# One scheduling block around a four-stage hybrid backbone kernel: its order is laid out on the library's timeline machine

## The chip, the cores and the metric

The kernel runs on one core of one Trainium2 chip. The metric is device time in microseconds (us), the median of several executions. One execution was also recorded by the hardware profiler; its rows are shown further down. Engines: PE is TensorE (matmuls), PEld its weight loads, DVE is VectorE, ACT is ScalarE, POOL is GpSimd, SP is SyncE, which issues the DMAs here.

## What is computed

Two layers (DEPTH = 2) act on 1024 latent tokens and 256 context tokens, width 1024, one sample, all float32.

```
h  = rmsnorm(x, g_pre) * (1 + scale) + shift      # adaLN; shift, scale, gate from silu(c) @ w_mod
layer 0: u = [ diff_attention(8 heads, 1280 keys) * silu(gate) ,  b * short_conv(c * h') * silu(gate) ]
layer 1: u = [ neighbourhood_attention(16 heads, 8x16 window + 256 context keys) * silu(gate) ,
               gated_linear_attention(4 heads, both directions) * silu(gate) ]
x  = x + gate * rmsnorm(u @ w_out, g_post)
```

Every product with a weight is done as three float32r matmuls on high and low parts (hi*hi, hi*lo, lo*hi), so that PE has much more to do than any other engine.

## The kernel before

`Kernel.run` calls the stages one after another: `setup` and `start` (conditioning, first norm, `h`), `layer0` (eight heads of differential attention, `diff_head`), `out0` (output projection and the second norm), `layer1` (gated linear attention, GLA, for four heads in `gla_head`, then neighbourhood attention, `na`, for 16 heads), and `out1` (last output projection).

The wide projections are cut in units of 1024 x 128 weights. A `Stream` hands them out: `ws.run(1)` inside an attention stage emits one projection step (24 matmuls into one of two PSUM buffers, `proj_chunk`, L445) between two pieces of attention work. That work is the cover: while a chain of small instructions runs on DVE, ACT and POOL, PE has a projection to go on with. Each weight unit is loaded by a DMA (L234), rounded on ACT (`whi`, L251), and its remainder is formed on POOL or DVE (`wlo`, L252).

What sets the order. The program is traced in the order in which the Python code emits it, and each instruction gets that place as its priority; `high_priority(offset=n)` moves what is emitted in it n places forward, a negative n back. When the context closes, the tile library plays the program on a timing simulator of the core: whenever an engine can take an instruction, it gets, of those whose operands and buffers are ready in the simulation, the one with the earliest priority. The order found this way becomes the fixed queue of each engine, with semaphores between the queues; on the chip each engine goes through its own queue in that order and waits where an operand is late. So the simulator's prices are not the time of anything on the chip, but they decide which of two instructions stands first in a queue. An order that was right at the simulator's prices makes an engine wait on the chip where an operand takes longer than priced.

The library has two such simulators. The default one is used for the kernel before; the library says of it that it leaves out the fixed cost of GpSimd's elementwise instructions. The other, the timeline machine, is described as the more detailed of the two, and recommended for a phase whose length GpSimd decides; its list of devices holds a read port and a write port that GpSimd and VectorE share. Both take an activation table as already loaded.

Three places carry offsets by hand: the K and Q products of the GLA levels (-6), the query split of the neighbourhood attention (`nqd`, +60) and the split of its turned probabilities (`pth`, `ptl`, -20). Only the last stage has an order of its own: in `out1` the queue of units is drained in `tc.manual_schedule()`, where every engine keeps the order of the code.

The GLA stage works on one head at a time. `gla_levels` goes through seven levels for each of the groups of tokens; a level exponentiates (ACT, L1138), multiplies K on POOL and Q on DVE (L1140), multiplies the two on PE (`gl`, L1145), and merges the result on DVE (L1154), while DVE updates the running sums (L1149). `gla_chunk` then carries the state S from chunk to chunk: a transpose, its high and low parts (`gkh` on ACT, `gkl` on DVE, L1205), the update `gu` (L1212) and the output `go` (L1229) on PE.

Of the kernel before, what the change touches and what calls it, by code (L numbers as in the profile page):

```python
# [40 lines left out]
class Stream:  # L41
# [39 lines left out]
    def run(self, n):  # L81
        for _ in range(n):
            if not self.step():
                return
# [15 lines left out]
class Kernel:  # L100
# [6 lines left out]
        return (ctx or self.ctx).enter_context(self.tc.tile_pool(name=name, bufs=bufs, **kw))  # L107

    def run(self):
        self.setup()  # L110
        with ExitStack() as es:
            self.hp = self.pool("hp", ctx=es)
            rope_es, out_es = ExitStack(), ExitStack()
            self.start(rope_es)
            conv_es = self.layer0(rope_es)
            self.layer1(self.out0(conv_es, out_es), out_es)
            with ExitStack() as es2:
                self.out1(es2)
# [1501 lines left out]
```

## Time and profile before

| | |
|---|---|
| median of 3 runs | 3096.65 us (3096.41 to 3098.51) |
| the profiled execution, its own time | 3092.35 us |
| its span, first to last instruction | 3090.6 us |
| granted PE clock, mean | 0.992 |
| instructions | 42514 |

The profile page gives the busy time of each engine, and the trace behind it answers by stretch, by tile, or by who waited for whom. A busy engine is not one at its peak: the ends of matmuls are modelled. An idle engine off the critical path costs nothing.

### The profile page before, as it was taken

To read this page: it belongs to the slowest core of one execution; us is meant where nothing else is said; L and a number is where in the kernel's file an instruction comes from. 1 tells how busy PE (TensorE), PEld (TensorE's weight loads), DVE (VectorE), ACT (ScalarE), POOL (GpSimd) and SP (SyncE) were. 2 spreads that over 40 slices of the span, in tenths; PEclk is the share of its full clock that TensorE was granted. 3 is DMA by queue.
4 is the path that set the end of the run, shared out by engine and by line. 5 is a ranking of instruction groups with operands and counts; after the bars stand their busy time and mean duration, and the time that the engine had idled before them with its cause. 6 is when DMAs were issued, how large, how long until landed. Compare 5 with 4: busy or idle time off the path is not lost. (4 is left out here: it accounts for less than half of the span.)

```text
span 3090.6 us, 42514 instructions
## 1 busy us (share of the span) xinstructions
PE 2935.1 (95%) x16244; PEld 2437.7 (79%) x16244; DVE 1909.9 (62%) x3276; ACT 1498.9 (48%) x2757; POOL 1025.9 (33%) x813
## 2 busy tenths in 40 slices
PE   6999999999999999999999998989899999999898
PEld 4788888888888888888877777778777888887686
DVE  5575757566565657565244778685836666667723
ACT  4453535354445445453344555555535555556522
POOL 2203130313021221205233334342435555556622
PEclk9999999999999999999999999999999999999999
DMA  6011111211020211116342112111131111113323
GB/s 227 28 51 50 49 45 35 65 34 54 28 72 28 65 35 42 43 50 208 96 159 81 42 42 63 48 55 59 52 99 31 47 49 44 43 44 98 117 77 123
DMA packets 236982, 206.59 MB, mean 67 GB/s; under 512 B 43591, under 2 KB 194538, under 8 KB 236778
## 3 DMA queue, kind: packets, MB, share of 16 engines
q1 hardware_dynamic: 236778, 203.87, 21.3%
q8 instruction: 128, 2.10, 0.3%
q14 instruction: 76, 0.62, 0.1%
HBM read 168.17 MB, written 35.67 MB: 66 GB/s over the span
## 5 line engine op out<-in xcount | busy, mean ns | idle before, releaser
L252 POOL TENSOR_TENSOR wlo<-wraw,whi 128x1024 fp32r<-128x1024 f32 x149 | 366.8, 2462 | 1075.6 <-ACT whi L251 994.9
L445 PE MATMUL pj<-hBh,whi 128*128 128x512 f32 (+1 forms) x1712 | 382.2, 352 | 1.4 <-ACT gk L1048 1.0
L445 PE MATMUL pj<-hBl,whi 128*128 128x512 f32 (+1 forms) x1712 | 368.0, 347 | 0.0
L445 PE MATMUL pj<-hBh,wlo 128*128 128x512 f32 (+1 forms) x1712 | 351.3, 344 | 0.0
L251 ACT CAST whi<-wraw 128x1024 fp32r<-128x1024 f32 x176 | 184.4, 1048 | 319.9 <-PE ops L761 190.2
L445 PEld LDWEIGHTS pj<-hBh,wlo 128*128 128x128 f32 x1712 | 277.3, 190 | 36.8
L445 PEld LDWEIGHTS pj<-hBl,whi 128*128 128x128 f32 x1712 | 277.0, 190 | 34.3
L445 PEld LDWEIGHTS pj<-hBh,whi 128*128 128x128 f32 x1712 | 273.0, 190 | 35.4 <-ACT gk L1048 1.2
L445 PE MATMUL pj<-hAh,whi 128*128 128x512 f32 x968 | 279.5, 410 | 18.9 <-ACT ropex L524 12.9
L445 PE MATMUL pj<-hAl,whi 128*128 128x512 f32 x968 | 255.3, 394 | 0.0
L599 DVE TENSOR_REDUCE st<-S 128x1 f32<-128x1280 f32 (+1 forms) x160 | 203.8, 1274 | 79.8 <-PE S L597 79.8
L445 PE MATMUL pj<-hAh,wlo 128*128 128x512 f32 x968 | 249.6, 393 | 0.0
L1451 POOL TENSOR_TENSOR np<-np,nst 128x640 f32<-128x640 f32 x128 | 166.7, 1305 | 192.6 <-DVE nst L1450 141.9
L601 ACT ACTIVATE p<-S,st 128x1280 f32<-128x1280 f32 (+1 forms) x160 | 186.1, 1163 | 85.1 <-DVE st L599 83.6
L445 PEld LDWEIGHTS pj<-hAh,whi 128*128 128x128 f32 x968 | 170.6, 191 | 52.6 <-ACT ropex L524 14.4
L445 PEld LDWEIGHTS pj<-hAh,wlo 128*128 128x128 f32 x968 | 180.4, 188 | 36.6
L445 PEld LDWEIGHTS pj<-hAl,whi 128*128 128x128 f32 x968 | 177.9, 189 | 34.5
L597 PE MATMUL S<-kst,qd 128*128 128x512 f32 (+1 forms) x832 | 193.6, 363 | 4.9 <-ACT p L601 3.5
L597 PEld LDWEIGHTS S<-kst,qd 128*128 128x128 f32 x832 | 137.8, 189 | 45.7 <-ACT p L601 25.2
L1447 DVE CUSTOM_DVE_ANT_0 np<-NS,nB 128x640 f32<-128x640 f32 x128 | 105.3, 823 | 90.5 <-PE NS L1444 84.7
L622 ACT CAST ath<-atr 128x512 fp32r<-128x512 f32 (+1 forms) x208 | 99.2, 505 | 117.2 <-PE atr L619 116.6
L1502 DVE TENSOR_TENSOR ptl<-ntr,pth 128x512 fp32r<-128x512 f32 (+2 forms) x224 | 117.5, 536 | 49.3 <-ACT pth L1501 45.6
(361 smaller groups left out, 6265.7 us busy)
## 6 DMA issues: line engine op xcount, KB each, us to landing
wraw<-in_ev_w_in_dram SPq DMA_DIRECT2D x64, 512.0 KB, 3.9
wraw<-in_od_w_in_dram SPq DMA_DIRECT2D x56, 512.0 KB, 3.7
wraw<-in_w_out_dram SPq DMA_DIRECT2D x55, 512.0 KB, 3.7
wraw<-in_w_mod_dram SPq DMA_DIRECT2D x48, 512.0 KB, 3.7
sgT<-gt SPq DMA_DIRECT2D x32, 256.0 KB, 2.0
uT<-sg SPq DMA_DIRECT2D x8, 640.0 KB, 4.5
nG<-in_rpbp_dram SPq DMA_DIRECT2D x128, 40.0 KB, 2.2
xt<-in_x_dram SPq DMA_DIRECT2D x8, 512.0 KB, 7.4
```

The lines of the kernel that those rows point to most:

```text
L251: nc.scalar.copy(out=hi, in_=u.raw)
L252: (nc.vector if u.lo_eng == "v" else nc.gpsimd).tensor_tensor(out=lo, in0=u.raw, in1=hi.bitcast(F32), op=ALU.subtract)
L445: nc.tensor.matmul(ps[:, 0:tn], lhsT=a[:, k, :], rhs=self.h_at(k, t0, tn)[b], start=n == 0, stop=n == 23)
L597: nc.tensor.matmul(S[:, c0:c0 + tn], lhsT=qd[:, 2 * m + part, P * qt:P * qt + P], rhs=self.kst[m][:, t0:t0 + tn], start=part == 0, stop=pa ...
L599: nc.vector.tensor_reduce(out=st[:, m:m + 1], in_=S[:, 0:n], axis=AX.X, op=ALU.max, negate=True)
L601: nc.scalar.activation(out=p[m][:, 0:n], in_=S[:, 0:n], func=AF.Exp, bias=st[:, m:m + 1], accum_out=st[:, 2 + m:3 + m])
L622: nc.scalar.copy(out=dh, in_=tv)
L1447: nc.vector.tensor_tensor_reduce(out=p, in0=S[:, z0:z0 + 640], in1=bias[2 * i + m][:, c0:c0 + 640], scale=1.0, scalar=3e38, op0=ALU.add, o ...
L1451: nc.gpsimd.tensor_tensor(out=p, in0=p, in1=st[:, 2:3].broadcast_to([P, 640]), op=ALU.mult)
L1502: nc.vector.tensor_tensor(out=lv[:, s:e], in0=tr[:, s:e], in1=hv[:, s:e].bitcast(F32), op=ALU.subtract)
```

## The change

`run` becomes a wrapper that opens one block around all of the work, and the old body moves unchanged to `work`. The library traces a block into a basic block of its own that is entered unconditionally and scheduled as a unit; with `schedule_with_timeline_sim=True` the block, and what is nested in it, is scheduled on the timeline machine, the rest of the context on the default one. Here nothing of the kernel lies outside. No operation, tile, pool size, offset or DMA is added or taken away in the source.

```diff
     def run(self):
+        with self.tc.block(schedule_with_timeline_sim=True):
+            self.work()
+
+    def work(self):
         self.setup()
         with ExitStack() as es:
             self.hp = self.pool("hp", ctx=es)
             rope_es, out_es = ExitStack(), ExitStack()
             self.start(rope_es)
             conv_es = self.layer0(rope_es)
             self.layer1(self.out0(conv_es, out_es), out_es)
             with ExitStack() as es2:
                 self.out1(es2)
```

## Rows read from the trace of the kernel before

**Rows 1.** The page: busy us, share of the span and instructions of each engine.
```profile
PE 2935.1 (95%) x16244; PEld 2437.7 (79%) x16244; DVE 1909.9 (62%) x3276; ACT 1498.9 (48%) x2757; POOL 1025.9 (33%) x813
```
**Rows 2.** Busy time by stage, whole core; columns are named in the first row.
```profile
core 0: us, PE busy (x) PEld busy (x) DVE busy (x) ACT busy (x) POOL busy (x), PEclk, DMA share, GB/s
0.00:152.00 152.00, 118.56 (x686) 90.90 (x687) 83.41 (x166) 65.68 (x111) 41.03 (x38) 0.96 0.38 130
152.00:1237.00 1085.00, 1074.13 (x6180) 896.78 (x6179) 693.37 (x1106) 519.13 (x836) 217.82 (x113) 1.00 0.15 46
1237.00:1580.00 343.00, 334.75 (x1683) 277.64 (x1684) 178.36 (x278) 150.36 (x233) 102.70 (x61) 0.98 0.34 111
1580.00:1720.00 140.00, 133.83 (x641) 110.73 (x639) 60.26 (x105) 59.16 (x99) 45.54 (x30) 0.98 0.28 84
1720.00:2250.00 530.00, 481.73 (x2702) 396.03 (x2702) 397.63 (x622) 300.25 (x628) 210.04 (x163) 1.00 0.17 52
2250.00:2780.00 530.00, 509.76 (x2948) 432.31 (x2947) 335.69 (x707) 277.64 (x598) 277.45 (x297) 1.00 0.20 51
2780.00:2931.00 151.00, 133.93 (x770) 111.38 (x769) 111.62 (x215) 89.63 (x186) 92.01 (x84) 0.98 0.31 98
2931.00:3058.00 127.00, 127.00 (x555) 104.90 (x555) 24.40 (x31) 26.50 (x45) 26.14 (x14) 0.99 0.31 103
3058.00:3091.00 33.00, 21.38 (x93) 17.00 (x91) 25.19 (x50) 10.58 (x24) 13.14 (x15) 0.90 0.32 128
```
**Rows 3.** What PE waited for, whole span: us in total, times, longest us.
```profile
PE gl L1145 <- DVE QL L1140: 28.5, 20, 1.8
PE NS L1443 <- DVE nqd L1432: 10.8, 8, 3.5
PE modps L279 <- DMA wraw<-in_w_mod_dram: 8.7, 1, 8.7
PE ntr L1492 <- POOL np L1451: 6.9, 11, 1.5
PE gu L1212 <- DVE gkl L1205: 6.4, 8, 1.4
```
**Rows 4.** The tile QL: its product on DVE, ns min/median/max.
```profile
L1140 DVE TENSOR_TENSOR QL<-QL,gq x56: 666/679/1786, 1730.2 to 2221.2; 128x512 f32<-128x512 f32 x56
```
**Rows 5.** Timeline 1908.7 to 1914, POOL, DVE and PE: start, duration, instruction [idle before].
```profile
1908.77 1.31 POOL L1188 TENSOR_TENSOR ql<-QF,qh 128x512 fp32r<-128x512 f32 x1 [1.29 <-ACT qh L1187]
...
1908.93 1.70 DVE L1140 TENSOR_TENSOR QL<-QL,gq 128x512 f32<-128x512 f32 x1
...
1910.78 1.13 PE L1145 MATMUL gl<-QL,gk 128*128 128x128 f32 x8 [1.79 <-DVE QL L1140]
...
1913.29 0.39 PE L445 MATMUL pj<-hAh,wlo 128*128 128x512 f32 x1
```
**Rows 6.** The groups of POOL by form: busy us, mean ns | idle before it.
```profile
L1223 POOL TENSOR_TENSOR gal<-att,gah 128x128 fp32r<-128x128 f32 x32 | 20.8, 659 | 18.1 <-ACT gah L1222 11.1 <-PE go L1229 6.9
L252 POOL TENSOR_TENSOR wlo<-wraw,whi 128x1024 fp32r<-128x1024 f32 x149 | 366.8, 2462 | 1075.6 <-ACT whi L251 994.9 <-PE pj L445 44.4 <-DVE Sl L1244 14.7
```
**Rows 7.** ACT_TABLE_LOAD before the logarithms: the groups of ACT by form.
```profile
L1105 ACT ACT_TABLE_LOAD x12 | 15.4, 1283 | 0.2
L317 ACT ACT_TABLE_LOAD x8 | 10.3, 1283 | 0.1
```
**Rows 8.** The chain of waits at its end: start, us, what.
```profile
2930.67 126.60 PE ops L761 x550
...
3086.27 0.75 DVE ox L925
3087.02 0.66 DVEq L1616
```

## The prediction, made before the changed kernel was run

> **What bounds the kernel now.** I read the page first: PE is busy 2935.1 us of a span of 3090.6, 95%, DVE 62%, ACT 48%, POOL 33% [rows 1]. The change alters no operation, so PE's work stays, and what an order can give or take is PE's idle time, 3090.6 - 2935.1 = 155.5 us. So the second view is busy time by stage, where the reader is to subtract PE's busy time from each stretch [rows 2]: 33.4 us idle in the start (0 to 152), 10.9 in the attention heads (152 to 1237, 1.0% of that stage), 8.3 and 6.2 in the output projection and the norms behind it (1237 to 1720), 48.3 in the gated linear attention (GLA, 1720 to 2250, 9.1%), 20.2 in the neighbourhood attention (2250 to 2780, 3.8%), 17.1 where it overlaps the last projection (2780 to 2931), none to 3058, and 11.6 in the tail. The third view is who PE waited for [rows 3]. The start waits for its first weights (8.7 us in one piece), and no order makes a first load faster. The tail runs in the order of the code in both kernels, and the chain of waits has one solid PE stretch of 126.6 us ahead of it [rows 8]. What is left for a planner is 48.3 + 20.2 + 17.1 = 85.6 us between 1720 and 2931.
>
> **What these waits are made of.** The largest, 28.5 us in 20 pieces, is PE's level product `gl` waiting for DVE's `QL` [rows 3]. The product for QL takes 679 ns at the median and up to 1786 [rows 4], though all 56 have one shape. One such case by the clock [rows 5]: POOL starts a 128x512 subtraction at 1908.77 that takes 1.31 us; DVE starts QL at 1908.93 and takes 1.70, that is 1.70 - 0.68 = 1.02 us more than the median, about what is left of POOL's instruction (1910.08 - 1908.93 = 1.15). PE waits 1.79 us for it, then goes through its small products, and at 1913.29 takes up a projection matmul. I read this as an inversion: the planner put `gl` ahead of a projection matmul because it thought QL done by then. The projection was under way before and after the wait, so its operands were there to fill it. A planner that knows of the collision, or of POOL's price, puts some of those matmuls first.
>
> **The change part by part.**
>
> 1. Operations: none added or removed, so no term. An order could add ACT table loads, 1283 ns each [rows 7]. There are 12 + 8 in front of logarithms, and the code has 3 groups x 4 heads of them on the one line and 8 heads on the other, so each logarithm already stands by itself; a new order can merge some, not add. I take 0; at most the 12 of L1105 fall away, 15.4 us of ACT, which is 52% idle, so the other end is near nothing too.
>
> 2. POOL's price. The trace has 659 ns for a 128x128 product on POOL and 2462 for 128x1024 [rows 6]: an eightfold width costs 3.7 times as much, and a straight line through the two leaves an intercept of 659 - (2462 - 659)/7 = 401 ns. That is an estimate of the part that the default simulator leaves out, for each of POOL's 813 instructions. The second number carries collisions with DVE, so 401 could be lower; below 0.2 us, half of it, the planner's picture of POOL changes little. It decides an order where POOL is last before PE: `ntr` behind `np`, 6.9 us in 11 pieces [rows 3].
>
> 3. The waits it can fill. I count those whose releaser is a POOL instruction, or a DVE one that POOL can have delayed, itself or through what stands ahead of it in DVE's queue: 28.5 (gl) + 10.8 (NS behind nqd) + 6.9 (ntr) + 6.4 (gu behind gkl) = 52.6 us [rows 3]. A matmul moved up into a wait is gone from the place where it stood, and there another chain may then be bare; cover is finite. From the trace I can't tell how much of it is given back: the ends are 0 (all of it) and 52.6 (none). I take the middle, 26 us: each wait is short (20 pieces in 28.5 us, 1.4 us each, three or four matmuls), and the case by the clock has a projection right behind it, but DVE is busy 397.6 of 530 us in GLA [rows 2], so it is close to being the next thing that is late. Wherever a wait for QL goes, DVE's own queue is what PE meets next: the merge and the running sums behind it on the same engine.
>
> 4. The stages that are full now. Attention runs at 1.0% idle and the last projection at 0 [rows 2]; a new order has little to win and can lose. Gain at most 10.9; loss, by the nearest stage with the same pattern (softmax chains with projections between), up to the 3.8% of the neighbourhood attention, 1085 x 2.8% = 30 us. I take 0, because there the chains have cover to spare: PE's queue hardly ever runs dry.
>
> 5. The block itself. It has an entry and an exit on each engine. No row shows one. The nearest small queue piece is the last one of the chain, 0.66 us [rows 8]; I take 0, as nothing lies outside the block, with a bound of twice 0.66 = 1.3 us. The DMA queue gets a new order as well: all weight loads are issued by SP ahead of need, and of PE's longest waits only that of the start names a DMA [rows 3]. Moved behind a late store, a weight load would cost what the first one does, 8.7 us [rows 3], once.
>
> Sum, against the profiled execution: 3092.35 - 26 = 3066.35. The median of the runs shown lies 4.30 above that execution (3096.65 - 3092.35), so on the median 3070.65, rounded 3071 (-0.8%).
>
> **The rivals.**
>
> A. The order moves the collisions instead of removing them. POOL and DVE have the same instructions to run in the same stage, 210 and 398 us busy in 530 [rows 2], so they must often meet; a new order draws new pairs, and other DVE products come out at 1.7 us. For: POOL is not the bound of any stage, which is the case the library recommends the machine for. Against: the largest wait sits on one pair of lines, 20 times, which looks like a fixed mistake and not like chance. Then the 48.3 us of GLA stay: 3096.65, within 6 us. The Trainium skill, "SBUF — State Buffer", section "Who interferes with whom", states that the shared port pair is an exclusive lock, that the loser is blocked for the whole instruction, and that issue order decides who blocks; by it a planner can choose the loser but not abolish the wait. The 1.02 us of the QL above agrees with a full block.
>
> B. Slower: cover is spent early. A simulation in which POOL and DVE take longer finds PE free more often, and hands it later projection steps sooner; they are limited by two PSUM buffers and by the weights' rounding, and when a head's softmax chain comes, less is left beside it. The place is the attention stage, 152 to 1237, which has the most to lose. The price is the neighbourhood stage's idle share instead of its own, the 30 us of part 4, with nothing gained in GLA: 3096.65 + 30 = 3127. It decides when PE's busy share in that stretch falls from 99.0% under 97%. For: three offsets in the source (-6, +60, -20) were set with the other prices in force, so under new prices they shift things that need no shift. Against: the code keeps two softmax units in flight there, and PE now waits for almost nothing in it.
>
> C. More than forecast: all of the 52.6 us is filled and nothing given back, 3096.65 - 52.6 = 3044. For: nearly all pieces are shorter than four matmuls. Against: DVE at 75% in GLA.
>
> **How the numbers follow.** A run of this kernel can tell a difference of about 0.2%, 6 us, from none. Chances: the forecast, a gain between 6 and 45 us, 0.40; C, 45 or more, 0.11; A, within 6 us, 0.15; B, slower by over 6 us, 0.34. So faster 0.51, same 0.15, slower 0.34. The likeliest case's own range is 3052 to 3090. The range of 8 in 10 goes down to C with a little beyond it, 3035, and up past B by its loss of 30 and one misplaced load of 8.7 with some more, to 3138.
>
> **What would show it.** In the changed profile, the waits of `gl` for QL should fall from 28.5 us to about half and PE's busy share in the GLA stretch rise from 90.9% to 93% or more; PE's total of busy time should stay within 1% of 2935. QL's median should stay 0.68 us; if the count of QL products over 1.2 us falls, the machine knows the collisions, and if it stays while PE's waits fall, it only placed the cover better. Attention should stay at 98% or more; if it drops, B is at work. The forecast is wrong if GLA's idle time stays near 48 us (A), or if the time comes out above 3097, and its mechanism is wrong if the gain comes from the start, the tail or the output projection.

## The result and the profile after

The changed kernel takes 3361.41 us (median of 3 runs, 3357.98 to 3378.40) against 3096.65: a ratio of 1.0868, interval 1.0811 to 1.0925. The forecast was 3071, with a range up to 3138. The profiled execution is the median run; its span is 3359.6 us, 269.0 more than before. Of the runs told of below, one execution of e3 came out in a slow state, 3561.34 us at a granted clock of 0.75 against 3046.00 to 3053.05 for its other three; e3's ratio leaves it out, its median of 3051.67 does not.

The page of after, with the rows of the slices that matter (busy tenths of PE in 40 slices, and its granted clock):

```profile
PE 3010.9 (90%) x16244; PEld 2549.6 (76%) x16244; DVE 1928.0 (57%) x3276; ACT 1490.8 (44%) x2757; POOL 1021.5 (30%) x813
PE   7988979798997979798799989889889999999898
PEclk9989989899998989899899999999999999998999
```

The five engines' counts of instructions are those of [rows 1], so no operation came in. PE's idle time went from 155.5 to 3359.6 - 3010.9 = 348.7 us, and its busy time up by 75.8. The digits fall in a pattern that repeats, in the first half: the attention heads.

I cut both spans at the first and last start of three PE tiles, `S` (attention heads), `gl` (GLA) and `NS` (neighbourhood attention), from the views of these tiles (us; the runs e2 to e11 are told below):

| | to first S | attention | to first gl | GLA | gap | NS | end |
|---|---|---|---|---|---|---|---|
| before | 120.8 | 1258.6 | 345.3 | 498.4 | 97.2 | 586.9 | 183.4 |
| after | 122.2 | 1479.0 | 322.7 | 518.2 | 117.3 | 620.8 | 179.4 |
| e2, first half only | 123.3 | 1453.9 | 366.6 | 501.6 | 96.6 | 587.1 | 184.4 |
| e8, default machine, cover first | 149.4 | 1488.0 | 344.1 | 497.9 | 96.7 | 586.9 | 181.8 |
| e4, PE window 1 | 127.3 | 1366.1 | 375.1 | 611.1 | 105.2 | 699.5 | 187.9 |
| e10, PE window 2 | 123.0 | 1266.0 | 338.3 | 494.3 | 93.9 | 566.0 | 178.8 |
| e5, PE window 4 | 121.4 | 1259.4 | 338.8 | 495.5 | 94.0 | 555.6 | 179.1 |
| e9, as e5, POOL cheaper | 121.4 | 1277.6 | 340.5 | 496.6 | 98.7 | 564.6 | 178.1 |
| e11, PE window 8 | 120.9 | 1268.3 | 348.4 | 489.1 | 96.9 | 563.3 | 181.3 |
| e6, PE window 16 | 124.2 | 1338.7 | 354.1 | 495.9 | 98.0 | 563.8 | 178.0 |
| e7, other windows 4 | 122.4 | 1476.6 | 322.9 | 530.5 | 113.2 | 619.1 | 179.3 |

Of the 269.0 us, 220.4 lie in the attention heads, 33.9 in the neighbourhood attention, 19.8 and 20.1 in GLA and behind it; 22.6 come back ahead of GLA. Busy time by stage, before (cut at the same landmarks), then after; columns as in [rows 2]:

```profile
121.00:1379.00 1258.00, 1240.32 (x7119) 1035.55 (x7119) 806.74 (x1290) 606.13 (x979) 248.76 (x132) 1.00 0.15 46
1725.00:2223.00 498.00, 449.73 (x2529) 369.81 (x2528) 384.18 (x597) 284.08 (x592) 197.53 (x154) 1.00 0.17 53
2320.00:2907.00 587.00, 556.68 (x3275) 472.69 (x3276) 411.85 (x856) 335.50 (x711) 335.04 (x348) 0.99 0.19 53
```

```profile
122.00:1601.00 1479.00, 1315.05 (x7224) 1118.82 (x7224) 857.27 (x1296) 612.23 (x995) 271.28 (x141) 0.93 0.14 44
152.00:1237.00 1085.00, 956.82 (x5253) 813.92 (x5251) 621.74 (x948) 444.02 (x720) 189.97 (x98) 0.93 0.13 40
1924.00:2442.00 518.00, 467.58 (x2590) 400.31 (x2589) 380.13 (x598) 282.98 (x595) 192.17 (x154) 0.97 0.17 51
2559.00:3180.00 621.00, 563.25 (x3278) 491.07 (x3277) 407.92 (x856) 336.02 (x712) 342.27 (x346) 0.97 0.19 51
```

In the attention heads idle time went from 17.7 to 164.0 us, and PE's busy time rose by 74.7 for 105 more matmuls. In the fixed stretch 152 to 1237 PE is busy for 88.2%, where rival B's line was 97%, and starts 5253 matmuls instead of 6180 [rows 2].

PE's waits after (columns as in [rows 3]; lines stand 4 lower than before), and the tile QL:

```profile
PE pj L449 <- ACT ropex L528: 78.4, 14, 6.5
PE S L601 <- ACT p L605: 35.9, 20, 3.0
PE NS L1447 <- DVE nst L1451: 18.4, 23, 1.6
...
PE nav L1473 <- DVE nu L1479: 15.9, 21, 1.3
...
PE gl L1149 <- ACT KL L1142: 8.4, 4, 2.8
...
PE gl L1149 <- DVE QL L1144: 7.8, 4, 2.7
PE gktr L1204 <- DVE KH L1181: 7.7, 4, 3.3
...
PE gl L1149 <- DVE g_u L1106: 6.5, 5, 3.1
L1144 DVE TENSOR_TENSOR QL<-QL,gq x56: 675/679/1777, 1931.7 to 2439.7; 128x512 f32<-128x512 f32 x56
```

The two waits of before that the first two of these rows grew from:

```profile
PE pj L445 <- ACT ropex L524: 12.9, 7, 5.3
...
PE S L597 <- ACT p L601: 3.5, 2, 3.3
```

Two things stand in these rows. The wait that the forecast was about did fall, from 28.5 to 7.8 us, and in the timeline of DVE only 2 of the 56 QL products take over 1.2 us, where 16 did before: the machine's order avoids most of the collisions of this pair. But behind them KL, KH and g_u are late instead, and GLA is no shorter; PE's idle time in it is 518 - 467.58 = 50.4 us, where it was 48.3. And two waits that were 12.9 (`ropex`) and 3.5 us (`p`) have become the largest.

Other products meet POOL instead. `qd`, the query split of the attention heads, on DVE, by form, in before, after and e5 (busy us, mean ns | idle before it):

```profile
L587 DVE TENSOR_TENSOR qd<-qf,qd 64x256 fp32r<-64x256 f32 x80 | 33.3, 417 | 10.6 <-ACT qd L586 9.2
L591 DVE TENSOR_TENSOR qd<-qf,qd 64x256 fp32r<-64x256 f32 x80 | 61.6, 770 | 1.7 <-ACT qd L590 0.5
L591 DVE TENSOR_TENSOR qd<-qf,qd 64x256 fp32r<-64x256 f32 x80 | 59.1, 739 | 4.1 <-ACT qd L590 2.5
```

Before, none of the 80 took over 423 ns. After, 22 take over 600 ns and one 2615, and each of the 22 runs beside a POOL instruction (as do 10 of the other 58). That is 28.3 us more, where the QL products gave back 14.1, and DVE as a whole is busy 18.1 us longer for the same 3276 instructions. It isn't the cause of the loss in the heads: e5 has nearly the same slow `qd`, and its heads take 1259.4 us.

One tail of a head, in PE's timeline of after (columns as in [rows 5]). The rows from 407.59 to 424.15 are the first and the last of two K steps of the *next* head:

```profile
407.59 1.97 PE L449 MATMUL pj<-hAh,whi 128*128 128x512 f32 x8
...
424.15 1.85 PE L449 MATMUL pj<-hBh,wlo 128*128 128x512 f32 x7
...
430.97 0.50 PE L601 MATMUL S<-kst,qd 128*128 128x256 f32 x2 [3.03 <-ACT p L605]
...
452.47 2.07 PE L449 MATMUL pj<-hBh,whi 128*128 128x256 f32 x8 [4.99 <-ACT ropex L528]
...
463.41 3.78 PE L449 MATMUL pj<-hAh,whi 128*128 128x512 f32 x8 [6.52 <-ACT ropex L528]
```

ACT in the same tail:

```profile
446.74 1.28 ACT L321 ACT_TABLE_LOAD   x1
...
449.38 1.28 ACT L322 ACT_TABLE_LOAD   x1
...
451.85 0.57 ACT L528 COPY ropex<-pj 128x512 f32<-128x512 f32 x1
...
462.77 0.58 ACT L528 COPY ropex<-pj 128x512 f32<-128x512 f32 x1 [0.79 <-DVE sg L649]
```

And a tail of before, on PE; here the last row is the first of the next head's K:

```profile
390.75 0.65 PE L643 MATMUL ms<-qf,onesD 128*128 128x256 f32 x2
391.05 2.18 PE L445 MATMUL pj<-hAh,wlo 128*128 128x512 f32 x8
...
401.88 2.00 PE L445 MATMUL pj<-hAh,whi 128*128 128x512 f32 x8
```

Before, projections of the convolution branch are left at the head's last `ms` (390.75), and PE runs through them until the next K at 401.88. After, they are used up. The planner has gone on to the next head's K, whose two steps fill both PSUM buffers; the copy that would free the first (`ropex`) runs only at 451.85, behind the last softmax work and the norm's two table loads. The copy of the second step comes 10.9 us later, at 462.77: in the code `ropex` shares its two SBUF buffers (tag `p0`) with the norm's `rs`, and the row names `sg`, which reads `rs`, as what the copy waited for. From 426 on the softmax chain is bare. Stretches of that tail:

```profile
407.60:424.00 16.40, 16.40 (x95) 14.30 (x95) 6.99 (x12) 5.06 (x8) 1.97 (x2) 1.00 0.14 40
426.50:447.00 20.50, 14.39 (x73) 11.83 (x74) 10.51 (x28) 9.15 (x22) 0.00 (x0) 0.83 0.00 1
447.00:463.40 16.40, 4.90 (x26) 4.29 (x25) 11.65 (x11) 7.63 (x8) 6.01 (x2) 0.65 0.00 0
463.40:470.00 6.60, 6.59 (x17) 5.21 (x18) 6.02 (x11) 1.16 (x3) 1.78 (x1) 0.57 0.60 179
470.00:490.00 20.00, 20.00 (x101) 17.01 (x100) 13.19 (x20) 4.85 (x10) 7.89 (x6) 1.00 0.08 27
```

PE idles 17.6 us between 426.5 and 463.4, and its granted clock (the column ahead of the last two) falls from 1.00 to 0.83, 0.65 and 0.57. So eight matmuls of the form that took 1.97 us at 407.59 take 3.78 at 463.41.

### The profile page after: what moved, and what is told of

Read it like the earlier page. It is cut to its first block, busy times and chain, and to the rows that moved or that the text cites. A ratio compares the mean times of both kernels' runs of the same rounds, so it can differ in the third digit from the quotient of the medians.

```text
span 3359.6 us, 42622 instructions
## 1 busy us (share of the span) xinstructions
PE 3010.9 (90%) x16244; PEld 2549.6 (76%) x16244; DVE 1928.0 (57%) x3276; ACT 1490.8 (44%) x2757; POOL 1021.5 (30%) x813
## 5 line engine op out<-in xcount | busy, mean ns | idle before, releaser
L256 POOL TENSOR_TENSOR wlo<-wraw,whi 128x1024 fp32r<-128x1024 f32 x149 | 381.6, 2562 | 958.5 <-ACT whi L255 692.2
L449 PE MATMUL pj<-hBh,whi 128*128 128x512 f32 (+1 forms) x1712 | 373.7, 358 | 58.7 <-ACT ropex L528 35.0
L449 PE MATMUL pj<-hBh,wlo 128*128 128x512 f32 (+1 forms) x1712 | 379.1, 350 | 0.0
L449 PEld LDWEIGHTS pj<-hBh,whi 128*128 128x128 f32 x1712 | 288.9, 197 | 110.0 <-ACT ropex L528 37.8
L449 PE MATMUL pj<-hAh,whi 128*128 128x512 f32 x968 | 270.0, 418 | 52.3 <-ACT ropex L528 43.4
L449 PEld LDWEIGHTS pj<-hBl,whi 128*128 128x128 f32 x1712 | 287.0, 198 | 36.7
L449 PE MATMUL pj<-hAh,wlo 128*128 128x512 f32 x968 | 259.5, 395 | 0.0
L449 PEld LDWEIGHTS pj<-hAh,whi 128*128 128x128 f32 x968 | 183.5, 200 | 94.7 <-ACT ropex L528 44.9
L601 PE MATMUL S<-kst,qd 128*128 128x512 f32 (+1 forms) x832 | 196.8, 368 | 36.1 <-ACT p L605 35.9
L532 POOL TENSOR_TENSOR ropex<-ropex,sin 128x512 f32<-128x512 f32 x32 | 57.7, 1802 | 450.4 <-DVE ropex L530 450.3
L601 PEld LDWEIGHTS S<-kst,qd 128*128 128x128 f32 x832 | 146.3, 199 | 62.7 <-ACT p L605 41.5
L627 DVE TENSOR_TENSOR atl<-atr,ath 128x512 fp32r<-128x512 f32 (+1 forms) x208 | 118.0, 584 | 122.6 <-ACT ath L626 120.9
```

The source lines that it names most:

```text
L256: (nc.vector if u.lo_eng == "v" else nc.gpsimd).tensor_tensor(out=lo, in0=u.raw, in1=hi.bitcast(F32), op=ALU.subtract)
L449: nc.tensor.matmul(ps[:, 0:tn], lhsT=a[:, k, :], rhs=self.h_at(k, t0, tn)[b], start=n == 0, stop=n == 23)
L532: nc.gpsimd.tensor_tensor(out=s, in0=s, in1=self.sin[:, t0:t0 + tn], op=ALU.mult)
L601: nc.tensor.matmul(S[:, c0:c0 + tn], lhsT=qd[:, 2 * m + part, P * qt:P * qt + P], rhs=self.kst[m][:, t0:t0 + tn], start=part == 0, stop=pa ...
L627: nc.vector.tensor_tensor(out=atl[:, g0:g0 + gn, P * qt:P * qt + P], in0=tv, in1=dh.bitcast(F32), op=ALU.subtract)
```

## The experiments

Theory W, formed on these rows: the timeline machine keeps an issue window for each engine, a number of instructions that stand in its queue beyond the one that runs; for PE it is 35. While a chain step isn't ready, the machine hands PE projection matmuls up to that number, and the step, once ready, goes behind them. In the rows of the tail a projection matmul is 1.81 us / 8 = 0.23 us from the next (407.59 to 409.40), so 35 of them are an estimated 8 us of delay for each step. The chain gets longer, more cover runs beside it, and none is left at the head's end. Rivals: the block itself (R1), and the prices of the timeline machine (R3). Where an expectation of e1 to e4 speaks of P2, it means W.

All windows are changed in one place, around the context in which the order is laid out; the instructions that run are the same:

```diff
+    depth, ET = TRN2Spec.ENG_ISSUE_QUEUE_DEPTH, mybir.EngineType
+    kept = dict(depth)
+    depth.update({ET.PE: 4})
     with tile.TileContext(nc) as tc:
         hybrid_kernel(tc, A, out)
+    depth.update(kept)
```

**e1, the block alone.**

```diff
-        with self.tc.block(schedule_with_timeline_sim=True):
+        with self.tc.block():
             self.work()
```

> The same block around all of the work, without the flag, so that the default simulator lays out the order. Its five queues hold the instructions in the same order as those of the kernel before. Theory P (the machine's order costs the time): 3097 us, within 6 of the kernel before. Rival R1 (the block itself costs, by its entry, its exit or its semaphores): near the changed kernel, 3361.

Measured: 3094.62 us, ratio 1.000 (0.9991 to 1.001). R1 is refuted: entry and exit cost nothing that shows.

**e2, the timeline machine for the first half.** The flagged block holds `setup`, `start` and `layer0`; what follows is laid out by the default machine. The edit is against the kernel before.

```diff
     def run(self):
-        self.setup()
-        with ExitStack() as es:
+        es, rope_es, out_es = ExitStack(), ExitStack(), ExitStack()
+        with self.tc.block(schedule_with_timeline_sim=True):
+            self.setup()
             self.hp = self.pool("hp", ctx=es)
-            rope_es, out_es = ExitStack(), ExitStack()
             self.start(rope_es)
             conv_es = self.layer0(rope_es)
+        with ExitStack():
             self.layer1(self.out0(conv_es, out_es), out_es)
...
```

> The block with the flag holds only the start and layer 0's attention heads (setup, start, layer0); the output projection and all of layer 1 are laid out by the default simulator. Attention ran from the first S to the last in 1259 us before and 1479 us in the changed kernel, 220 of the 265 us. Theory P1 (the loss is in the heads): 3097 + 220 = 3317, plus up to 20 us for what may no longer overlap across the block's border. Rival R2 (the loss is spread over all stages): about 42% of it, 3210.

Measured: 3313.41 us, ratio 1.0711 (1.0695 to 1.0727). The attention heads take 1453.9 us, 195.3 more than before, and GLA and the neighbourhood attention stay within 3.2 us of theirs. So most of the loss is made in the attention heads, and needs no other part of the kernel.

**e3, e5: PE's window 4.** One kernel, run twice; the profile told of here is that of e5.

> The changed kernel, with one number of the timeline machine altered while the order is laid out: PE's issue window, how many instructions its queue takes before they are done, 4 instead of 35. Nothing else differs. In PE's queue of a head 54 projection matmuls stand between the last full-width S and the head's norm (0 in the changed kernel, 47 in the kernel before). Theory P2 (the window lets projections run ahead of the chain's instructions, and the cover is spent before the head's end): attention back to under 1285 us from first to last S, the whole 3060 to 3130. Rival R3 (the machine's prices of GpSimd and VectorE make the order bad, whatever the window): within 60 us of 3361.

> The changed kernel with one number of the timeline machine altered while it lays the block out: PE's issue window is 4 instructions and not 35. It is the kernel of e3 again, for a profile that can be set beside that of before. Theory W (the window lets PE take projection matmuls far ahead of the softmax chain): 3040 to 3062 us; the attention heads take within 15 us of the 1259 us that they take before, first to last S; PE waits for ropex under 20 us where the changed kernel has 78. If the mechanism of the forecast is alive beside it, the gain against before lies in GLA and the neighbourhood attention: gl waits for QL under 15 us (before 28.5), and GLA's stretch is shorter by 10 us or more. Rival: the gain comes from the start or the attention heads, and GLA takes its 498 us as before.

Measured: e3 3051.67 us, ratio 0.9857 (0.9840 to 0.9875); e5 3047.92 us, ratio 0.9845 (0.9830 to 0.9860). One number of the planner takes away the whole loss and 1.5% more: this is the version that beats both kernels. The 19.8 and 33.9 us of GLA and the neighbourhood attention are gone as well, but how the window had made those was not traced. R3 falls as the cause of the loss, since all prices of the timeline machine are in force. The busy time of e5, its stages, and some of its waits:

```profile
PE 2893.6 (95%) x16244; PEld 2455.1 (81%) x16244; DVE 1953.9 (64%) x3276; ACT 1490.3 (49%) x2757; POOL 1014.8 (33%) x813
121.00:1381.00 1260.00, 1223.29 (x7134) 1051.48 (x7135) 851.36 (x1287) 601.85 (x977) 234.95 (x129) 0.99 0.15 46
1720.00:2215.00 495.00, 452.99 (x2538) 378.63 (x2537) 392.72 (x595) 279.79 (x590) 192.97 (x152) 0.99 0.17 53
2309.00:2865.00 556.00, 541.49 (x3296) 474.97 (x3296) 403.33 (x857) 337.08 (x713) 337.70 (x346) 0.99 0.21 58
```

```profile
PE pj L449 <- ACT ropex L528: 24.5, 8, 6.3
PE gl L1149 <- DVE QL L1144: 17.1, 14, 2.5
...
PE NS L1447 <- DVE nqd L1436: 2.4, 2, 1.6
...
PE ntr L1496 <- POOL np L1455: 1.6, 2, 1.2
```

The heads take their 1259 us again, as expected, but the wait for ropex is 24.5 and not under 20, and PE idles there for 36.7 us where it was 17.7; it is busy for 17.0 us less. The gain lies elsewhere than I expected: GLA is 2.9 us shorter, not 10, and QL's wait is 17.1. The neighbourhood attention is 31.3 us shorter, two thirds of the span's 46.8: about half is idle time (30.0 to 14.4), where `nqd` and `np` went from 10.8 and 6.9 [rows 3] to 2.4 and 1.6; the other half is PE's own busy time, 15.7 us less. Over the whole span that is nearly everything: PE's busy time fell by 2935.1 - 2893.6 = 41.5 us for the same 16244 matmuls, at a mean granted clock of 0.990 against 0.992, and its idle time by 5.3. So on balance the gain of this version is not a gain in waits, and no run here explains it.

**e4, PE's window 1.**

> The same with a window of 1. In PE's queue 52 projection matmuls stand in a head's tail. Theory P2: as with 4 or a little better or worse in the stages of layer 1, 3050 to 3130 in all; if the machine's better prices are worth what was forecast, it lies below 3097. Rival R3: within 60 us of 3361.

Measured: 3473.52 us, ratio 1.1226 (1.1208 to 1.1245): the worst of all, a miss. Cover is left at the end of the heads (table below), so this is another loss, and it lies in all stages with chains. PE's largest waits in e4:

```profile
PE gl L1149 <- DVE QL L1144: 70.8, 41, 3.6
PE nav L1473 <- DVE nu L1479: 55.0, 61, 1.5
PE S L601 <- ACT p L605: 43.0, 36, 4.7
```

**e6, e10, e11: PE's window 16, 2 and 8.**

> As e5 with a window of 16. In the order of PE's queue, of a typical head's 360 projection matmuls 50 are then left at its first S, and at its last softmax matmul 48 of the next head are already done (before: 103 and 56 left; changed kernel: 48 of the next head are done before the first S). Theory W: the loss grows with the share of the head that is left bare, so between e3 and the changed kernel: 3100 to 3250 us, the attention heads 1300 to 1420. Rival (the window acts only through another thing that 4 happens to avoid): within 20 us of 3052 or within 30 of 3361.

> As e5 with a window of 2, between e5 (4: 3048) and e4 (1: 3474). In PE's queue 88 projection matmuls of a typical head are left at its last S and 31 at its last softmax matmul (e5: 77 and 23; e4: 114 and 62). Theory W alone (only run-ahead costs): 3035 to 3065 us, attention heads 1250 to 1270. Rival V (a narrow window costs by itself: with fewer matmuls in flight PE is slower in the machine than on the chip, so the machine leaves too little cover between a chain's steps, and the chip's PE waits for them): over 3100, with PE's waits of gl for QL over 40 us, and most of the loss in GLA and the neighbourhood attention.

> As e5 with a window of 8. In PE's queue 72 projection matmuls of a typical head are left at its last S, 17 at its first and none at its last softmax matmul (e5: 77, 34 and 23; e6, window 16: 50, and 28 and 48 of the next head done). Theory W: the loss begins where the cover runs out before the tail's end, so a small one: 3050 to 3090 us, attention heads 1260 to 1300. Rival (a step: the loss is there as soon as the tail's last matmul is bare): 3100 or more, near e6's 3154.

Measured: window 16, 3153.51 us, ratio 1.0190 (1.0175 to 1.0205); window 2, 3068.33, ratio 0.9918 (0.9903 to 0.9933); window 8, 3074.34, ratio 0.9932 (0.9918 to 0.9946). Beside them, counted in PE's queue of each kernel, the projection matmuls of a typical head that are left ahead of the next head's K, at its last 512-wide S and at the first and the last `ms` (below zero: so many of the next head are done already; 48 are two K steps; where an expectation says first or last S, it means the first of these places):

| PE window | left at last wide S | at first ms | at last ms | attention, us | total, us |
|---|---|---|---|---|---|
| before (default machine) | 103 | 59 | 56 | 1258.6 | 3096.65 |
| 1 | 114 | 65 | 62 | 1366.1 | 3473.52 |
| 2 | 88 | 40 | 31 | 1266.0 | 3068.33 |
| 4 | 77 | 34 | 23 | 1259.4 | 3047.92 |
| 8 | 72 | 17 | -6 | 1268.3 | 3074.34 |
| 16 | 50 | -28 | -48 | 1338.7 | 3153.51 |
| 35 (after) | -48 | -48 | -48 | 1479.0 | 3361.41 |
| e8, below (default machine, cover first) | -37 | -48 | -48 | 1488.0 | 3345.81 |

From 2 to 35 the attention heads grow as the cover runs out earlier: hardly where it lasts to the last `ms`, by 80 us where it ends before the first, by 220 where it ends before the last wide S. That is W's order of loss. The steps inside the machine's simulation were not recorded: that a chain step goes behind up to 35 matmuls there is inferred from this order. Window 2 missed its bounds by 3 us, but didn't bring the loss of rival V, which expected over 3100 and QL waits over 40. So the step between 1 and 2 (405 us) is not a gradual thing, and its cause stays open.

**e7, the windows of the other engines 4, PE's 35.**

```diff
-    depth.update({ET.PE: 4})
+    depth.update({e: 4 for e in depth if e != ET.PE})
```

> As e5, but the window is 4 for ACT, DVE, POOL and SP, and PE keeps 35. Theory W (only PE's window does the harm): 3361 us within 40, attention heads 1440 to 1520. Rival (the window of any engine lets the fill overtake the chain, ACT's above all, since ropex stands behind softmax work there): under 3250.

Measured: 3366.78 us, ratio 1.0878 (1.0862 to 1.0894), attention 1476.6. Only PE's window does it.

**e8, the default machine with cover first.** The kernel before, without a block; the one call in `diff_head` that emits the projection steps beside the softmax units is moved forward:

```diff
-            ws.run(1 + qt if qp < 4 else 0)
+            with self.tc.high_priority(offset=1000):
+                ws.run(1 + qt if qp < 4 else 0)
```

> The kernel before, laid out by the default machine without a block; only the call that emits the projection steps beside a differential attention head is put under a priority higher by 1000, so that the planner takes them as soon as they are ready. In PE's queue 37 matmuls of the next head are then done before the first S of a head, nearly as in the changed kernel (48). The other engines' prices and windows are those of before. Theory W (it is the order of cover against chain that costs, whatever machine makes it): 3230 to 3400 us, attention heads 1390 to 1500, PE waits for ropex over 40 us. Rival (the timeline machine does something else as well, in the order of ACT or DVE): under 3150, attention heads under 1310.

Measured: 3345.81 us, ratio 1.0811 (1.0793 to 1.0829). Its attention stage and its largest waits:

```profile
149.00:1637.00 1488.00, 1319.48 (x7158) 1090.90 (x7156) 825.17 (x1291) 608.41 (x989) 245.67 (x139) 0.95 0.14 42
```

```profile
PE pj L445 <- ACT ropex L524: 77.6, 16, 5.6
PE S L597 <- ACT p L601: 35.6, 37, 3.0
PE gl L1146 <- DVE QL L1141: 28.6, 20, 1.8
PE atr L619 <- DVE p L607: 22.8, 24, 1.6
```

Without the timeline machine, its prices or its window, an order that takes cover early gives the signature of the changed kernel: the wait for ropex (77.6 against 78.4), for p (35.6 against 35.9), busy time (1319 against 1315) and nearly the clock (0.95 against 0.93). GLA is as before, with QL's 28.6. Another 28.6 us of its loss lie ahead of the first S, where the changed kernel lost nothing, so the totals agree partly by chance; the attention stage is the comparison that counts. This run shows the cause apart from the machine: it is the order of cover against chain in the heads. Which share is due to the next head's K standing in both buffers was not tried.

**e9, POOL cheaper in the machine.** As e5, and POOL's fixed costs set to 0 while the order is laid out (`pool` holds the two numbers as they were):

```diff
+    TRN2Spec.GPSIMD_Q7_LAUNCH_NS = 0
+    TRN2Spec.GPSIMD_OP_FIXED_NS_AND_CYCLES_PER_ELEMENT = {k: (0, v[1]) for k, v in pool["GPSIMD_OP_FIXED_NS_AND_CYCLES_PER_ELEMENT"].items()}
```

> As e5 (PE's issue window 4), and while the block is laid out the timeline machine also prices every POOL instruction without its fixed part (the launch and the fixed cost per operation are set to 0; the part that grows with the width stays). The instructions that run are the same, in another order. In e5 the neighbourhood attention takes 556 us, first to last NS, against 587 before, and PE's waits for nqd, np and nu there are 7.3 against 24.7. Theory F (what is left of the forecast: it is POOL's price that places these chains better): without the price the gain goes, 570 to 590 us for that stage and 3065 to 3090 in all. Rival O (the machine's order of PE with a narrow window is better whatever POOL costs in it): 550 to 562 us for that stage, and within 10 of 3048 in all.

Measured: 3079.31 us, ratio 0.9951 (0.9939 to 0.9964). The total is where theory F had it, 31.4 us over e5, but the place is not: 18.2 us of it in the attention heads, where POOL has 129 instructions in e5's stretch, and 9.0 in the neighbourhood attention (564.6, between the two expectations). QL's wait is smaller than in e5 at the cheaper price:

```profile
PE pj L449 <- ACT ropex L528: 33.6, 14, 5.4
...
PE gl L1149 <- DVE QL L1144: 9.5, 15, 1.8
```

So the fixed part of POOL's price is worth about 1% to this planner, through many places, and not through the pair of lines on which the forecast stood.

## Why the prediction was wrong

The step that failed is part 4: "I take 0, because there the chains have cover to spare", with a loss of at most 30 us. The measured term is +220.4. It failed twice. The cover was to spare because the default machine's order left it at the head's end: 56 matmuls by the table, some 11 us in the tail shown. That is a property of the order, and the order is what the change replaces. And the bound came from the nearest stage with chains, the neighbourhood attention at 3.8% idle, whose order was made by the same old planner; it says how bad that planner's order is elsewhere, not how bad another planner's can be. The other bound, a head's chain with the cover taken away, I didn't work out. Nor was the reserve ample: [rows 3] skips the second line of its view, `pj` waiting for `ropex`, 12.9 us in 7 pieces, all of them in the heads, where PE's whole idle time was 17.7. It is the line that grew to 78.4. (It skips `nav` waiting for DVE's `nu` as well, 7.4 us, which part 3 did not count.)

Rival B had the mechanism (cover spent early; little left beside the softmax chain; limited by two PSUM buffers), the place and the sign. Its reason was off: it put the early cover down to POOL and DVE being priced longer. With these prices and a window of 4 the loss is gone (e5), and without them it is there when the source puts cover first (e8); the reason was PE's window, which the prediction did not look at, though it read both machines for their prices. Its size, 30, was wrong by the same bound as part 4.

Part 3 was right in its object and wrong in its worth. QL's wait fell by 20.7 us, more than the half that was forecast, and `nqd` and `np` left the list of the largest; yet GLA took 19.8 us more. The signs that the prediction set say the same: PE's busy share from the first to the last `gl` is 90.3% as before, not 93% or more, and its idle time there stays near 48 us (50.4). In the runs with narrower windows QL's wait is 17.1 (e5), 17.0 (e11), 9.2 (e10) and 1.9 (e6), and GLA 495.5, 489.1, 494.3 and 495.9 against 498.4: 3 to 9 us, without relation to that wait. The prediction said why this can be (a matmul moved into a wait is gone elsewhere, and DVE "is close to being the next thing that is late"), and then took the middle. e8 shows the same from the other side, with QL at 28.6 and GLA at 497.9. Of rival A two parts hold: the waits moved, and the new order drew new pairs. Of the slow QL products 14 of 16 went, and 22 slow `qd` products came, in another stage.

Part 2 took POOL's price as the thing that decides. By e9 it decides 31 us, more than the 26 of the sum, but most of it in the attention heads. Parts 1 and 5 held: the instruction counts are the same, ACT's table loads are 41 in both by the views of its lines, the block costs nothing (e1), and no weight load grew into a large wait.

Of the signs named, "Attention should stay at 98% or more; if it drops, B is at work" did its work: 88.2%. PE's busy time was to stay within 1% of 2935; it is up 2.6%, with a mean granted clock of 0.949 against 0.992. With e5, where it fell by 41.5 us, this takes away the premise that an order can give or take idle time alone.

## What to carry to other kernels

When a change replaces the planner, an even stage is not safe: ask what its order keeps in reserve, and bound the loss by the chain with that reserve gone, not by another stage of the old order. A planner that runs ahead on the busiest engine spends cover as soon as it is ready; where a chain ends each period, look at what is left at its last instruction. And a wait that falls is worth only what the stage's length says: read the stage from first to last instruction before counting it.

## What the runs showed that I had not expected

The clock added to the loss. While PE is full its granted clock is 1.00, the 2.4 GHz level; in the tail shown it is 0.83 over a stretch with 6.1 us of idle time in 20.5, 0.65 over the next with 11.5 in 16.4, and 0.57 over the 6.6 us after that, though PE is busy throughout those: a mean between the two levels that puts most of it at 1.2 GHz. From 470 to 490 it is back at 1.00. Over the heads the mean is 0.93, and of the 220 us some 146 are idle time and 75 busy time. An estimated 18 of the 75 are the 105 more matmuls (at before's mean, 1240.32 us / 7119 = 0.174 us each). So some 57 are left for the same matmuls taking longer, two fifths on top of the idle time. That the clock makes up all of the 57 isn't shown, since e5 changed the busy time at nearly the same clock.

A planner can be too short-sighted as well as too far-sighted: window 1 costs 12.3%, window 35 8.7%, and 4 gains 1.5%.
